# Neighbourhood attention: five score banks, three value banks whose results are copied out, and strict groups of products

## The chip, the cores and the metric

The kernel runs on one core of one Trainium2 chip. The metric is the device time of one execution in microseconds. The kernel before took 3622.86 us in the median of three runs (3616.02 to 3626.13).

A core has a matrix engine (TensorE, PE in the profile, with its weight loads shown apart as PEld), a vector engine (VectorE, DVE), a scalar engine (ScalarE, ACT), a general engine (GpSimd, POOL) and DMA queues, one fed by SyncE (SP) and one by GpSimd. Each engine runs its own instructions in their order and waits for others through semaphores. TensorE writes its products into PSUM, of which this kernel uses eight banks of 128x512 float32 in the stage in question; everything else lies in SBUF.

## What is computed

The reference is a two-layer backbone over 2048 latent tokens on a grid of 32 rows by 64 columns, with 256 context tokens in front. Layer 0 has latent attention and gated linear attention. Layer 1, with the stage in question, is neighbourhood attention with 16 heads of 64:

```python
def neighborhood_attention(q, k, v, k_ctx, v_ctx, rpb):
    ...
    def one_row(args):
        qr, r = args
        r_start = jnp.clip(r - kr // 2, 0, rows - kr)
        kb = lax.dynamic_slice_in_dim(kg, r_start, kr, axis=1)
        vb = lax.dynamic_slice_in_dim(vg, r_start, kr, axis=1)
        ...
        s_lat = jnp.einsum('bqhd,brkhd->bhqrk', qr, kb, preferred_element_type=jnp.float32) * scale
        s_lat = s_lat + bias.astype(jnp.float32)[None]
        s_lat = jnp.where(col_mask[None, None, :, None, :], s_lat, -jnp.inf).reshape(bsz, h, GRID_W, kr * GRID_W)
        s_ctx = jnp.einsum('bqhd,bchd->bhqc', qr, k_ctx, preferred_element_type=jnp.float32) * scale
        p = jax.nn.softmax(jnp.concatenate([s_lat, s_ctx], axis=-1), axis=-1).astype(v.dtype)
        o = jnp.einsum('bhqk,bkhd->bqhd', p[..., :kr * GRID_W], vb.reshape(bsz, kr * GRID_W, h, d))
        return o + jnp.einsum('bhqc,bchd->bqhd', p[..., kr * GRID_W:], v_ctx)
```

Every query sees a window of 8 by 16 latent tokens around it, with a bias table and a mask, and all 256 context tokens. The output is gated, projected and added to the stream.

## The kernel before, in words

The change touches `odd_attention` alone. It works through eight head pairs j; heads 2j and 2j+1 sit side by side in the partitions of the result.

A head pair has 20 steps. A context step ("c", n) makes the scores of the 512 queries of block n against the 256 context tokens: four products pairs (lines 1540 and 1541, the second of which adds the low parts and the maximum), one PSUM bank "st" each, and ACT takes the Exp out of each bank into an SBUF tile "opt". A latent step ("l", n) takes 128 latent keys against the rectangle of queries that can see them: two banks, one for each head; DVE adds the bias table out of the bank into an "opt" tile (line 1701, two or more rectangles for a tile), and ACT takes the Exp in place. The order of the steps is c0, c1, l0 to l3, c2, l4 to l7, c3, l8 to l15.

Every step has a tail, appended to a list `pend`. When six stand there, `flush(4)` runs the four oldest. A context tail opens a value bank "o" with eight products (line 1552) and DVE adds its two halves into the sums of the denominator (line 1560, two adds of 128x512, both inputs in SBUF). A latent tail adds value products into one or two value banks (line 1570), and POOL adds the tile into the sums (line 1576). The tail products are issued behind the last score product that stands before them; the score products after a flush are not tied to it, so the scheduler can place them among the tails.

The latent steps 7, 11 and 15 complete blocks 0, 1, and 2 with 3. Each completed block is put into `late` with a count of 2, and at the end of the second flush counted from there `finish_block` calls `finish` (lines 884 to 900): two products sum the denominators into a bank of the "st" ring (line 889); ACT takes Ln into "rl" and Exp into "rc"; DVE runs three operations of 128x512 (line 894 multiplies in the bank, line 895 writes the refined reciprocal into "rc", line 896 multiplies the value bank by it); the POOL queue stores the result (line 899).

Between the steps stand loads on the SP queue (keys by chunks of 512 tokens, queries, tables, values of the next head pair) and, at step 10, the masking of the next head pair's two tables by POOL (line 1533, two operations of 128x1034), issued behind the last POOL add at that place.

The "st" ring has four banks and the "o" ring four; they are all eight. In the last head pair the steps also split the output weights (`out_s`), and the projection of the first output tile (`first`) is woven in between the last flushes. The output projection follows.

Of the kernel before, what the change touches and what calls it, by code (L numbers as in the profile page):

```python
# [13 lines left out]
ALU = mybir.AluOpType  # L14
# [3 lines left out]
P = 128  # L18
# [70 lines left out]
class Kern:  # L89
# [1379 lines left out]
    def odd_attention(self, out, right, left, wout):  # L1469
# [4 lines left out]
        with ExitStack() as es:  # L1474
# [5 lines left out]
            for g in range(4):  # L1480
                steps += [("l", 4 * g + c) for c in range(4)]
                if g < 2:
                    steps.append(("c", g + 2))
            bank = lambda: self.tl(pp, [P, 512], "st", bufs=4)
            exps = lambda shape=[P, 2, 512], dt=F32: self.tl(ep, shape, "opt", dt, bufs=11)

            def qtile(j, i, part):
# [57 lines left out]
                return [acc[bb // 2][:, i].rearrange("p r c -> p (r c)")[:, (bb % 2) * 512 : (bb % 2) * 512 + 512] for i in range(2)]  # L1545

            def tail_ctx(n, pts, j, V, O, acc):
                O[n] = self.tl(pp, [P, 8, 64], "o", bufs=4)
                o = O[n][:].rearrange("p r c -> p (r c)")
                for u in range(2):  # L1550
                    for i in range(2):
                        mm = nc.tensor.matmul(o[i * 64 : i * 64 + 64, :], V[:, u, i * 64 : i * 64 + 64], pts[i][:, u, :],  # L1552
                                              start=u == 0, stop=False, skip_group_check=True)
                if n % 2 == 0:
                    if n == 0 and j % 2 == 0:
                        acc[0] = self.tl(left, [P, 2, 16, 64], "wo0", bufs=1)
                    else:
                        acc[n // 2] = self.tl(rp, [P, 2, 16, 64], f"oacc{n // 2}", bufs=1)
                for i, a in enumerate(sums(acc, n)):
                    nc.vector.tensor_tensor(out=a, in0=pts[i][:, 0, :], in1=pts[i][:, 1, :], op=ALU.add)  # L1560
                return mm

            def tail(n, pts, j, V, O, acc):
                g, c = divmod(n, 4)
                (r0, nr), (c0, w) = rect("k", g, c)
                done = {7: [0], 11: [1], 15: [2, 3]}.get(n, [])
                for bb in range(r0 // 8, (r0 + nr - 1) // 8 + 1):
                    a0, a1 = max(r0, bb * 8), min(r0 + nr, bb * 8 + 8)
                    for i in range(2):
                        mm = nc.tensor.matmul(O[bb][i * 64 : i * 64 + 64, a0 - bb * 8 : a1 - bb * 8, c0 : c0 + w],  # L1570
                                              V[:, NCT + n, i * 64 : i * 64 + 64], pts[:, i, a0 - r0 : a1 - r0, :],
                                              start=False, stop=bb in done, skip_group_check=True)
                for hf in range(r0 // 16, (r0 + nr - 1) // 16 + 1):
                    a0, a1 = max(r0, hf * 16), min(r0 + nr, hf * 16 + 16)
                    a = acc[hf][:, :, a0 - hf * 16 : a1 - hf * 16, c0 : c0 + w]
                    self.psum = nc.gpsimd.tensor_tensor(out=a, in0=a, in1=pts[:, :, a0 - r0 : a1 - r0, :], op=ALU.add)  # L1576
                late.extend([2, bb, j, O, acc] for bb in done)
                return mm

            def finish_block(bb, j, O, acc):  # L1580
                return self.finish(O.pop(bb)[:].rearrange("p r c -> p (r c)"), sums(acc, bb), None,
                                   self.RT1[j, :, bb * 512 : bb * 512 + 512], 512, fp, pp, ("st", 4), lp, (2, 3), nc.gpsimd)

            def weights():

# [50 lines left out]
            pend, late, OA = [], [], {}  # L1636
            all_k, most_k = slice(0, KD), slice(0, KD - 1)

            def flush(n):

                mm = None
                for f, *a in pend[:n]:
                    mm = f(*a)
                del pend[:n]
                for x in late:
                    x[0] -= 1
                for x in [x for x in late if x[0] <= 0]:
                    late.remove(x)
                    rc = finish_block(*x[1:])
                    if x[1:3] == [0, 7]:  # L1650
                        k = KD - 1
                        nc.gpsimd.tensor_tensor(out=r0[:, k, :], in0=rc[:, :P], in1=z0[:, k, :], op=ALU.mult)
                        self.project_split(r0[:, k, :], hi0[:, k, :], lo0[:, k, :])
                return mm

            for j in range(8):
                OA[j] = {}, {}
                for s, (kind, n) in enumerate(steps):
# [18 lines left out]
                    pts = exps() if kind == "l" else [exps(), exps()]  # L1677
                    if s in CHUNK and (j, s) not in ((0, 0), (7, 16)):
                        kt.append(chunk(j + (s == 16), CHUNK[s]))
                    for i in range(2):  # L1680
                        q1, q2 = Q[j, i]
                        if kind == "c":
                            for u in range(2):
                                ps = bank()
                                ks, qs = slice(u * P, u * P + P), slice(n * 512, n * 512 + 512)
                                mm = scores(ps[:], kc[j][0][:, i, ks], kc[j][1][:65, i, ks], q1[:, qs], q2[:65, qs])
                                ex = self.act(pts[i][:, u, :], ps[:], AF.Exp)
                            continue
                        k1, k2 = (k[:, i, c * P : c * P + P] for k in kt[0])
                        (r0_, nr), (c0, w) = rect("k", g, c)  # L1690
                        ps = bank()
                        a, m, d = even(c0, w)
                        pt = pts[:, i, : nr * w].rearrange("p (r c) -> p r c", r=nr)
                        ps = ps[:, : nr * m].rearrange("p (r c) -> p r c", r=nr)
                        q1, q2 = (q[:].rearrange("d (r c) -> d r c", r=32)[:, r0_ : r0_ + nr, a : a + m] for q in (q1, q2))
                        mm = scores(ps, k1, k2[:65], q1, q2[:65])
                        ps = ps[:, :, d : d + w]
                        for ro, ri, rn in pieces("k", 0, g, r0_, nr):
                            for co, ci, cn in pieces("k", 1, c, c0, w):
                                d = slice(ro, ro + rn), slice(co, co + cn)  # L1700
                                nc.vector.tensor_tensor(out=pt[:, d[0], d[1]], in0=ps[:, d[0], d[1]],  # L1701
                                                        in1=tabs[j][i][:, ri : ri + rn, ci : ci + cn], op=ALU.add)
                    if kind == "l" and c == 3:
                        kt.pop(0)
                    if kind == "l":
# [18 lines left out]
                        self.project_split(r0[:, most_k, :], hi0[:, most_k, :], lo0[:, most_k, :])  # L1724
                    if len(pend) == 6:
                        with self.tc.issue_after(mm.ins):
                            flush(4)
            for _ in out_s:
                pass
            y = lambda: self.tl(fp, [P, 512], "rc", bufs=3)  # L1730
# [144 lines left out]
```

## Time and profile before

| | |
|---|---|
| Median of three runs | 3622.86 us |
| The profiled execution | 3621.41 us |
| its span | 3619.6 us |
| its mean granted TensorE clock | 0.987 |
| Layer 1 attention in it | about 3032 to 3425 us |
| Output projection in it | from there to the end |

The page gives each engine's busy time and its share of the span. The windows give the same for a stretch: start and end, length, then busy time with the number of records for each engine, the granted clock of TensorE (1.00 is full), the busy share of the DMA engines and what they moved. A row of the timeline has its start, its length (of a run of like instructions where several are joined), engine, line, operation, result and operands, shape, and the count; the idle time before it and what ended it stand in brackets. A row of the waits has the engine, what it was about to write and the line, what it waited for, then the total in us, how many times, and the longest. A row of the groups has the form, the count, the busy time, the mean of one in ns, and the idle time before. Matmuls are pipelined, so neighbouring rows overlap, and the pace is read from start to start.

### The profile page before, as it was taken

The numbers are of one execution on the slowest core, as the hardware profiler recorded it, in microseconds if no ns is written. First come the engines' busy times: TensorE is split into PE (matmuls) and PEld (weight loads), VectorE is DVE, ScalarE is ACT, GpSimd is POOL, SyncE is SP. The second block draws the span as 40 slices with busy tenths as digits, with TensorE's granted clock in tenths as the row PEclk, the third lists the DMA queues.
The fourth block names the chain that finished last, engine by engine and source line by source line (L and its number), as shares of the span: only waits on it lengthen the run. The fifth ranks groups of instructions, "written<-read, shape, count | busy, mean of one in ns | idle before, by whom it ended". The sixth has DMA issues, their size and how long they took to land. (4 is left out here: it accounts for less than half of the span.)

```text
span 3619.6 us, 51689 instructions
## 1 busy us (share of the span) xinstructions
PE 3525.1 (97%) x18260; PEld 2737.6 (76%) x18260; DVE 2377.0 (66%) x4876; ACT 1429.4 (39%) x2705; POOL 1213.9 (34%) x1346
## 2 busy tenths in 40 slices
PE   8999999999999999999999999999999999999898
PEld 6988998888886666656667878888888886555577
DVE  4677665888886676697664344454587874677821
ACT  5545551111115555556553134444422223555510
POOL 1433430111011222212312233333444445677743
PEclk9999999999999999999999999999999999999999
DMA  7555462222243342424524544456644438778654
GB/s 253 151 155 155 140 197 92 90 76 84 72 115 83 91 108 72 108 79 134 157 89 144 172 158 129 144 147 192 212 139 127 131 124 205 210 210 221 185 178 145
DMA packets 396428, 513.63 MB, mean 142 GB/s; under 512 B 61229, under 2 KB 275197, under 8 KB 390266
## 3 DMA queue, kind: packets, MB, share of 16 engines
q1 hardware_dynamic: 358282, 426.94, 40.9%
q0 software_dynamic: 20512, 58.02, 5.6%
q10 hardware_dynamic: 17376, 25.37, 2.0%
q8 instruction: 145, 2.38, 0.3%
q14 instruction: 113, 0.93, 0.1%
HBM read 330.61 MB, written 179.59 MB: 141 GB/s over the span
## 5 line engine op out<-in xcount | busy, mean ns | idle before, releaser
L1007 DVE TENSOR_TENSOR acc<-acc,apt 128x512 f32<-128x512 f32 x512 | 376.0, 763 | 152.8 <-ACT apt L106 149.2
L666 DVE TENSOR_REDUCE mm<-mx 128x1 f32<-128x512 f32 (+1 forms) x656 | 393.0, 629 | 91.3 <-PE mx L665 83.1
L106 ACT ACTIVATE apt<-st 128x512 f32<-128x512 f32 (+1 forms) x592 | 342.9, 593 | 269.4 <-PE st L1018 224.4
L958 PE MATMUL av<-apt,av 128*64 128x512 f32 (+1 forms) x1184 | 269.2, 592 | 0.0
L1016 PE MATMUL st<-aq,akh 97*128 97x512 f32 x576 | 246.7, 428 | 0.6 <-ACT apt L106 0.6
L665 PE MATMUL mx<-mk,mq 96*128 96x512 f32 (+1 forms) x656 | 238.9, 373 | 0.0
L1017 PE MATMUL st<-aq,akh 96*128 96x512 f32 x576 | 229.1, 398 | 0.0
L1018 PE MATMUL st<-aq,akl 96*128 96x512 f32 x576 | 228.5, 397 | 0.0
L1443 DVE CUSTOM_DVE_ANT_1 mx<-mx,mtab 128x465 f32<-128x465 f32 (+14 forms) x576 | 184.0, 339 | 49.0 <-PE mx L1437 33.9
L106 ACT ACTIVATE opt<-opt 128x930 f32<-128x930 f32 (+9 forms) x144 | 119.1, 829 | 240.9 <-POOL opt L1741 136.4
L106 ACT ACTIVATE u<-gm 128x352 f32<-128x352 f32 (+1 forms) x144 | 70.3, 495 | 358.0 <-PE gm L131 207.4
L1701 DVE TENSOR_TENSOR opt<-st,tab 128x64 f32<-128x64 f32 (+10 forms) x576 | 143.3, 316 | 84.8 <-PE st L1541 47.4
L958 PEld LDWEIGHTS av<-apt,av 128*64 128x64 f32 x1184 | 79.8, 137 | 152.0 <-issue 149.7
L1576 POOL TENSOR_TENSOR oacc<-oacc,opt 128x682 f32<-128x682 f32 (+9 forms) x144 | 173.2, 1227 | 38.3 <-ACT opt L106 37.1
L1016 PEld LDWEIGHTS st<-aq,akh 97*128 97x128 f32 x576 | 108.9, 189 | 72.8 <-issue 43.4
L665 PEld LDWEIGHTS mx<-mk,mq 96*128 96x128 f32 x656 | 122.9, 189 | 11.7
L1018 PEld LDWEIGHTS st<-aq,akl 96*128 96x128 f32 x576 | 110.1, 191 | 25.2
L1540 PE MATMUL st<-q,kt 128*128 128x480 f32 (+5 forms) x256 | 100.3, 394 | 24.6 <-DVE opt L1701 20.0
L1017 PEld LDWEIGHTS st<-aq,akh 96*128 96x128 f32 x576 | 110.5, 192 | 17.6
L106 ACT ACTIVATE x<-px,modB,modA 128x128 f32<-128x128 f32 x272 | 99.1, 468 | 59.3 <-PE px L335 37.0
L129 PE MATMUL gm<-w0h,hhi 128*128 128x512 f32 x288 | 115.6, 401 | 2.3 <-DVE hhi L347 2.3
L129 PE MATMUL gm<-w1h,hhi 128*128 128x512 f32 x288 | 116.6, 405 | 0.0
(585 smaller groups left out, 9922.9 us busy)
## 6 DMA issues: line engine op xcount, KB each, us to landing
q<-Q SPq DMA_DIRECT2D x48, 512.0 KB
H<-x ACTq DMA_DIRECT2D x36, 512.0 KB
adaw<-ada_w SPq DMA_DIRECT2D x64, 256.0 KB
x<-H SPq DMA_DIRECT2D x32, 512.0 KB
K1t<-okt POOLq DMA_DIRECT2D x32, 512.0 KB, 6.7
kt<-K1t SPq DMA_DIRECT2D x32, 512.0 KB
mtab<-rpb_q SPq DMA_DIRECT2D x16, 899.0 KB
QT<-qkhl SPq DMA_DIRECT2D x36, 384.0 KB
```

The costliest lines, as they stand in the source:

```text
L106: return self.nc.scalar.activation(out, in_, func, **kw)
L129: self.nc.tensor.matmul(out, lh(k), rh(k), start=j == 0, stop=False)
L665: mm = nc.tensor.matmul(ps[:, :w], q[:A_QK, (t % 6) * P : (t % 6) * P + P], k[:A_QK, k0 : k0 + w], start=True, stop=True)
L666: nc.vector.tensor_reduce(out=m[:, t, n : n + 1], in_=ps[:, :w], axis=AX.X, op=ALU.max)
L958: nc.tensor.matmul(O[j, nb][i * 64 : i * 64 + 64, :w], V[j, kt // TT][:, kt % TT, i * 64 : i * 64 + 64], pts[i][:, :w], start=n == 0, stop ...
L1007: self.add = nc.vector.tensor_tensor(out=acc[i][:, :w], in0=a[:, :w], in1=pts[i][:, :w], op=ALU.add)
L1016: nc.tensor.matmul(ps[:, :w], kh[: A_QK + 1, i, kq], qh[: A_QK + 1, :w], start=True, stop=False)
L1017: nc.tensor.matmul(ps[:, :w], kh[:A_QK, i, kq], ql[:A_QK, :w], start=False, stop=False)
L1018: mm = nc.tensor.matmul(ps[:, :w], kl[:A_QK, i, kq], qh[:A_QK, :w], start=False, stop=True)
L1443: nc.vector.tensor_tensor_reduce(out=s, in0=s, in1=tb[:, ri : ri + rn, ci : ci + cn], scale=1.0, scalar=-3e38, op0=ALU.add, op1=ALU.max, a ...
L1576: self.psum = nc.gpsimd.tensor_tensor(out=a, in0=a, in1=pts[:, :, a0 - r0 : a1 - r0, :], op=ALU.add)
L1701: nc.vector.tensor_tensor(out=pt[:, d[0], d[1]], in0=ps[:, d[0], d[1]], in1=tabs[j][i][:, ri : ri + rn, ci : ci + cn], op=ALU.add)
```

## The change

Four things change. The rings: five "st" banks and three "o" banks. The end of a block: with its last value product ACT copies the value bank into an "rc" tile, and the bank is free for the next block; the denominator is worked on at the start of the next flush, in one "st" bank that the first two DVE operations rewrite in place, and the third multiplies the copy. The groups: the first scores after a flush are tied to the flush's last product (`behind`), and the first flush of all runs three tails, so that later groups end with l7, l11 and l15, the last product of a block; a flush of one tail is added after the loop. The tiles of the first output tile's projection come from the ring "rl".

In the order of the instructions that results, DVE has the two adds of c2 (line 1560) just behind the table adds of l5, and POOL has the table masks (line 1533) behind l3's add and ahead of those of l4; before, they stood behind l4's adds. The order of the loads on the SP queue is the same.

```diff
-            bank = lambda: self.tl(pp, [P, 512], "st", bufs=4)
+            bank = lambda: self.tl(pp, [P, 512], "st", bufs=5)
...
-                O[n] = self.tl(pp, [P, 8, 64], "o", bufs=4)
+                O[n] = self.tl(pp, [P, 8, 64], "o", bufs=3)
...
-                late.extend([2, bb, j, O, acc] for bb in done)
+                for bb in done:
+                    r = self.tl(fp, [P, 512], "rc", bufs=3)
+                    self.act(r[:], O.pop(bb)[:].rearrange("p r c -> p (r c)"))
+                    late.append((bb, j, r, acc))
                 return mm
 
-            def finish_block(bb, j, O, acc):
-                return self.finish(O.pop(bb)[:].rearrange("p r c -> p (r c)"), sums(acc, bb), None,
-                                   self.RT1[j, :, bb * 512 : bb * 512 + 512], 512, fp, pp, ("st", 4), lp, (2, 3), nc.gpsimd)
+            def finish_block(bb, j, r, acc):
+                den = bank()
+                for h, a in enumerate(sums(acc, bb)):
+                    nc.tensor.matmul(den[h * 64 : h * 64 + 64, :], self.mtwos[:], a, start=True, stop=True)
+                q = self.tl(lp, [P, 512], "rl", bufs=2)
+                self.act(q[:], den[:], AF.Ln, scale=-1.0)
+                self.act(q[:], q[:], AF.Exp, scale=-1.0)
+                nc.vector.tensor_tensor(out=den[:], in0=den[:], in1=q[:], op=ALU.mult)
+                nc.vector.scalar_tensor_tensor(out=den[:], in0=den[:], scalar=2.0, in1=q[:], op0=ALU.add, op1=ALU.mult)
+                nc.vector.tensor_tensor(out=r[:], in0=den[:], in1=r[:], op=ALU.mult)
+                nc.gpsimd.dma_start(self.RT1[j, :, bb * 512 : bb * 512 + 512], r[:])
+                return r
...
             def flush(n):
 
                 mm = None
+                for x in late:
+                    rc = finish_block(*x)
+                    if x[:2] == (0, 7):
+                        k = KD - 1
+                        nc.gpsimd.tensor_tensor(out=r0[:, k, :], in0=rc[:, :P], in1=z0[:, k, :], op=ALU.mult)
+                        self.project_split(r0[:, k, :], hi0[:, k, :], lo0[:, k, :])
+                late.clear()
                 for f, *a in pend[:n]:
                     mm = f(*a)
                 del pend[:n]
-                for x in late:
-                    x[0] -= 1
-                for x in [x for x in late if x[0] <= 0]:
-                    late.remove(x)
-                    rc = finish_block(*x[1:])
...
+                    es2 = ExitStack()
+                    if behind is not None:
+                        es2.enter_context(self.tc.issue_after(behind.ins))
+                        behind = None
                     for i in range(2):
...
+                    es2.close()
...
                     if len(pend) == 6:
                         with self.tc.issue_after(mm.ins):
-                            flush(4)
+                            behind = flush(3 if (j, s) == (0, 5) else 4)
+            with self.tc.issue_after(mm.ins):
+                mm = flush(1)
...
-            steps_of = lambda o, hi, lo, x: self.project_steps(hi, lo, x, gate, wout, bank, y, out[o * P : o * P + P, :])
-            first = steps_of(0, hi0, lo0, x0)
+            steps_of = lambda o, hi, lo, x, y=y: self.project_steps(hi, lo, x, gate, wout, bank, y, out[o * P : o * P + P, :])
+            first = steps_of(0, hi0, lo0, x0, lambda: self.tl(lp, [P, 512], "rl", bufs=2))
```

More of the change, by code (lines that the diff above doesn't have):

```diff
@@ L1635, in odd_attention @@
             out_w, out_s = weights(), split()
-            pend, late, OA = [], [], {}
+            pend, late, OA, behind = [], [], {}, None
             all_k, most_k = slice(0, KD), slice(0, KD - 1)
@@ L1644, in flush @@
                 del pend[:n]
-                for x in late:
-                    x[0] -= 1
-                for x in [x for x in late if x[0] <= 0]:
-                    late.remove(x)
-                    rc = finish_block(*x[1:])
[L1650 to L1653, printed above, removed]
                 return mm
```

## The prediction, made before the changed kernel ran

> **What bounds the kernel now.** I began with the page: TensorE (PE) is the bound of the whole span, and no other engine is near it.
>
> ```profile
> span 3619.6 us, 51689 instructions
> ...
> PE 3525.1 (97%) x18260; PEld 2737.6 (76%) x18260; DVE 2377.0 (66%) x4876; ACT 1429.4 (39%) x2705; POOL 1213.9 (34%) x1346
> ```
>
> The change touches the neighbourhood attention of layer 1 alone. In the timeline this runs from about 3032 to 3425 us, 8 head pairs one after the other. So I cut it at the same instruction of every head pair, the 48 value products that follow the last score group, and read the windows between those cuts.
>
> ```profile
> core 0: us, PE busy (x) PEld busy (x) DVE busy (x) ACT busy (x) POOL busy (x), PEclk, DMA share, GB/s
> 3076.10:3124.88 48.78, 46.86 (x305) 28.87 (x304) 30.26 (x89) 25.09 (x40) 31.63 (x28) 0.96 0.84 214
> 3124.88:3173.07 48.19, 46.28 (x306) 27.83 (x305) 32.76 (x94) 25.58 (x41) 34.74 (x31) 0.96 0.78 209
> 3173.07:3219.79 46.72, 44.81 (x307) 27.38 (x306) 35.47 (x94) 25.59 (x41) 32.73 (x30) 1.00 0.81 214
> 3219.79:3268.15 48.36, 46.43 (x305) 27.73 (x304) 32.63 (x94) 25.55 (x41) 36.12 (x32) 0.96 0.79 208
> 3268.15:3316.41 48.26, 46.35 (x306) 27.86 (x305) 32.71 (x94) 25.60 (x41) 34.67 (x31) 0.96 0.80 207
> 3316.41:3361.96 45.55, 44.04 (x306) 27.52 (x305) 35.63 (x94) 25.64 (x41) 32.55 (x29) 1.00 0.83 224
> 3361.96:3425.00 63.04, 54.16 (x367) 33.49 (x367) 55.72 (x124) 36.66 (x62) 44.24 (x40) 0.95 0.54 168
> ```
>
> Six steady head pairs take 47.64 us in the mean (3361.96 less 3076.10, over 6). Four show a granted clock of 0.96 and take 48.4 us in the mean; two show 1.00 and take 46.1. The last window is another case: VectorE (DVE) is busy 55.7 of 63.0 us there.
>
> "PE busy 96%" hides the loss, because pipelined ends overlap. I therefore compared, in the undisturbed head pair at 3173.07, the time of each stretch of score products with the columns in it.
>
> ```profile
> 3177.65 0.29 PE L1540 MATMUL st<-q,kt 128*128 128x264 f32 x1
> ...
> 3182.11 0.40 PE L1540 MATMUL st<-q,kc 128*128 128x512 f32 x1
> 3182.35 0.39 PE L1541 MATMUL st<-q,kc 65*128 65x512 f32 x1
> 3182.58 0.40 PE L1540 MATMUL st<-q,kc 128*128 128x512 f32 x1
> ...
> 3183.14 2.28 PE L1570 MATMUL o<-opt,ov 128*64 128x72 f32 x32
> 3185.25 1.03 PE L889 MATMUL st<-wo,mtwos 128*64 128x512 f32 x4
> 3186.21 0.40 PE L1540 MATMUL st<-q,kt 128*128 128x288 f32 x1
> ...
> 3190.79 1.94 PE L1552 MATMUL o<-opt,ov 128*64 128x512 f32 x8
> ...
> 3199.54 0.32 PE L1540 MATMUL st<-q,kt 128*128 128x360 f32 x1
> ...
> 3203.13 1.32 PE L1570 MATMUL o<-opt,ov 128*64 128x248 f32 x16
> ...
> 3216.15 0.49 PE L1540 MATMUL st<-q,kt 128*128 128x480 f32 x1
> ...
> 3219.78 3.02 PE L1570 MATMUL o<-opt,ov 128*64 128x72 f32 x48
> ```
>
> A pair of score products (L1540 and L1541) of 512 columns repeats every 0.47 us (3182.11 to 3182.58), 0.92 ns a column. One head pair has 20064 columns of scores (16 context tiles of 512; 32 latent tiles of 264 to 480), so 18.4 us at that pace. The stretches take longer. 3186.21 to 3190.79 is 4.58 us for 2688 columns, worth 2.5: 2.1 lost, with a denominator bank (L889) held. 3199.54 to 3203.13 is 3.59 us for 2640 columns, worth 2.4: 1.2 lost. 3216.15 to 3219.78 is 3.63 us for 2912 columns, worth 2.7: 1.0 lost. Counted so, the score stretches of this head pair lose 7.1 us, the turns from one kind of work to the other included; 46.72 less 7.1 leaves 39.6 us of work. The waits name who holds the bank.
>
> ```profile
> PEld st L1540 <- issue: 4.3, 9, 0.8
> PEld st L1540 <- PE st L1541: 3.6, 7, 0.8
> ...
> PE st L1540 <- DVE opt L1701: 1.5, 4, 0.5
> PEld st L1540 <- ACT opt L106: 1.2, 3, 0.5
> PEld st L1540 <- PE st L889: 0.8, 1, 0.8
> ```
>
> A score product waits for the DVE add of the table (L1701) or the Exp (L106) that empties a bank of the ring of four. The issue waits, 9 of them, are mostly the turns from value products back to scores, some 0.3 us each.
>
> **The change, part by part.** *A fifth score bank, and groups that are strict.* The static order of PE shows, per head pair, exactly five score groups and five tail groups of four steps; the order before turns seven times from values to scores. Two turns less are 0.6 us of the sum below. With letters for the new groups (scores, then what holds banks there): A = latent 9 to 12, nothing held; B = latent 13 to 15 and context 0, one denominator bank held; C = context 1, latent 0 to 2, nothing; D = latent 3, context 2, latent 4 and 5, nothing; E = latent 6, 7, context 3, latent 8, two denominator banks held. Groups A, C and D are like the stretches that lose 1.0 to 1.2 with four banks; with a fifth I take a third off: 0.7 each. B is like the stretch that lost 2.1, with four banks free where that had three: 1.7. E has three free, but its context step needs no DVE: 1.8, between 0.7 (denominators done early) and 4.1 (all six DVE operations ahead of its adds, 6 times 0.68). Sum 5.5, the five turns included, against 7.1 with seven: -1.5 us per head pair, rounded down, from -2.7 (E at 0.7) to +0.7 (E at 4.1).
>
> *The copy.* ScalarE (ACT) gets four copies of 128x512 from PSUM per head pair. No such copy is in the trace; the nearest rows are two ACT operations of that size from PSUM.
>
> ```profile
> L106 ACT ACTIVATE rl<-st 128x512 f32<-128x512 f32 x29 | 17.2, 593 | 46.0 <-PE st L889 46.0
> L106 ACT ACTIVATE opt<-st 128x512 f32<-128x512 f32 x112 | 60.3, 603 | 29.9 <-PE st L1541 29.9
> L1560 DVE TENSOR_TENSOR oacc<-opt 128x512 f32<-128x512 f32 x44 | 47.1, 1082 | 0.1
> ```
>
> Four times 0.60 is 2.4 us on an engine busy 25.6 of 46.7: nothing on the path while that slack covers it; without it, 0.6 us behind each of three block ends, 1.8. What queues behind a copy is the next Exp, and behind that the value products of its step. The value bank comes free at the copy, so three are enough; the old order held it to L896, whose successor reads the copy. The "rc" ring has three buffers, so block 3's copy must wait until the store of block 0 has landed.
>
> ```profile
> RT<-rc POOLq DMA_DIRECT2D x29, 256.0 KB, 6.3
> ```
>
> Block 0 is stored in group A and block 3 copied at the end of group C, two groups later, some 18 us: 6.3 us of landing is hidden, price 0; uncovered it would hold ACT for the rest of a landing.
>
> *The denominators earlier.* They are issued one flush sooner. PE sees the same four products; what can be late is their sums, made by GpSimd (POOL, L1576) and by L1560. From 0 to 2 us per head pair; I take 0, since they stand behind three tails in the order of PE.
>
> *What moves beside GpSimd's masks.* In the order of DVE, the two adds of context step 2 (L1560) come just behind the table adds of latent 5; in POOL's order the masks (L1533) now stand before latent 4's adds, where before they were behind them.
>
> ```profile
> 3205.20 4.77 POOL L1533 TENSOR_TENSOR tab<-tab,maskk 128x1034 f32<-128x1034 f32 x2
> 3209.91 4.21 POOL L1576 TENSOR_TENSOR oacc<-oacc,opt 128x682 f32<-128x682 f32 x4
> ...
> 3210.81 3.87 DVE L1560 TENSOR_TENSOR oacc<-opt 128x512 f32<-128x512 f32 x1
> ...
> 3215.11 0.68 DVE L1560 TENSOR_TENSOR oacc<-opt 128x512 f32<-128x512 f32 x1
> ```
>
> The same add takes 0.68 us alone and 3.87 us beside four POOL operations that run back to back; the mean of 44 is 1.08. It ends within 0.6 us of the last of the four: it is shut out while POOL runs. Beside the masks, each of the two adds can wait for the rest of a mask of 2.4 us, 1.7 us more than alone, or for a whole train, 3.2 more; together 0 to 6.4. DVE has 11 us of slack in a head pair, yet the table adds of group E are queued behind these two. In the sum I take 0, as most adds run at 0.68; the rest is a rival. [...]
>
> *The rest.* The first flush, the extra one at the end and the "rl" tiles of the first output tile: once each, under 1 us. The first head pair and the last gain little: the last is bound by DVE. So 6 head pairs and half of one more: 6.5 times -1.5 is -9.8 us.
>
> *The clock.* The four head pairs at 0.96 are 2.3 us longer than the two at 1.00.
>
> ```profile
> 3142.92 3.10 PE L1552 MATMUL o<-opt,ov 128*64 128x512 f32 x8
> ```
>
> The same eight products take 1.94 us in the row at 3190.79: a stretch at a lower clock, right behind the score group that loses 2.1 us. That group's tiles fall into C and D, which lose less; B and E remain as triggers. I let two of the four go: -4.6, between -9.2 and +4.6 (all six). [...]
>
> Sum: 3619.6 + 1.8 around it = 3621.4; less 9.8 and 4.6 gives 3607.0. This run lies 1.5 us under the median of the runs shown.
>
> **The rivals.** *The lock (B).* The two adds of context step 2 meet the masks. For it: the new order of both queues, and the row of 3.87 us. Against it: DVE's slack, and most adds at 0.68. Price: one add waits for a mask (1.7), the other for a train (3.2), 4.9 us of DVE ahead of group E's table adds; 1.3 of it lies in waits that E has anyway, and 3.6 less the gain of 1.5 is +2.1 per head pair. The two head pairs without a dip then have one too: +4.6. 3621.4 + 6.5 times 2.1 + 4.6 = 3639.7, from 3626 (one mask only, 0.5 per head pair) to 3652 (4 us). It decides from the point where the two adds cost 2.8 us of DVE, 1.5 and the 1.3.
>
> *Strict groups give it back (C).* The order before could fill a wait for a bank with value products; the strict one cannot. For it: the loss gathers in B and E, each behind denominators. E at 3.3 instead of 1.8 takes the whole gain: 3621, from 3613 to 3636. Against it: the group that lost 1.2 had no denominator at all, only four banks.
>
> *ACT waits for a store (D).* The fourth copy waits for a landing, and ACT's Exps behind it. Against it: 18 us where 6.3 are needed. Were the landing 4 us late, 4 less 1.5 is 2.5 per head pair: 3638.
>
> **How the numbers follow.** A, the forecast, 0.45, own range 3594 to 3614; B 0.42; C 0.09; D 0.04. A measurement of this kernel can tell about 0.3%, 11 us, from no change: faster is under 3612, slower over 3634. A lies under 3612 nine times in ten: 0.41. B lies over 3634 four times in five, D nearly always, C one time in ten: 0.39. The rest is 0.20. The range 3588 to 3644 leaves out a little of A (all dips gone and more than 2 us per head pair) and three tenths of B, under 2 in 10.
>
> **What would show it.** Right: steady head pairs of 45 to 46.5 us, a granted clock of 1.00 in more of them, seven turns from values to scores become five, L1540's waits on L1701 smaller per head pair. The lock: L1560's mean well over 1.08 us, with DVE rows of 2 to 4 us beside L1533. C: waits on L889's banks and on L1701 in groups B and E that add up to 5 us or more. D: an ACT copy waiting for the store. I am wrong if the steady head pair stays at 47.6 or more with L1560 unchanged, or if the time moves outside the attention, which the change should leave alone.

## The result, and the profile after

The changed kernel is slower. Its median over six runs is 3635.32 us (3631.99 to 3644.48) against 3620.46 us for the kernel before in the same series; the ratio is 1.0044, 95% interval 1.0033 to 1.0055, some 16 us. The forecast was 3607. The profiled execution has a span of 3633.0 us, 13.4 more than before.

The windows of the changed kernel, cut at the start of group E (latent 6) of six head pairs in a row; columns as in the prediction.

```profile
core 0: us, PE busy (x) PEld busy (x) DVE busy (x) ACT busy (x) POOL busy (x), PEclk, DMA share, GB/s
3109.71:3162.58 52.87, 49.23 (x306) 32.77 (x305) 32.46 (x94) 27.88 (x45) 34.30 (x31) 0.87 0.71 190
3162.58:3210.36 47.78, 45.17 (x305) 29.34 (x304) 31.34 (x92) 27.59 (x45) 33.87 (x30) 0.96 0.80 210
3210.36:3260.53 50.17, 46.80 (x306) 30.44 (x305) 31.90 (x94) 27.59 (x45) 33.87 (x30) 0.93 0.75 200
3260.53:3306.46 45.93, 43.61 (x306) 28.51 (x305) 31.29 (x92) 27.48 (x45) 33.19 (x30) 1.00 0.81 214
3306.46:3356.73 50.27, 46.14 (x306) 30.70 (x305) 32.89 (x93) 27.65 (x45) 34.29 (x31) 0.93 0.73 199
3356.73:3406.11 49.38, 46.07 (x306) 31.00 (x305) 37.35 (x96) 29.88 (x49) 33.08 (x30) 0.93 0.57 176
```

Six head pairs take 296.40 us, 49.4 each. Before, six successive starts of the nearest stretch (second half of latent 7, 3112.49 to 3396.27) gave 47.3 each. That is +2.1 a head pair where -1.5 was forecast, +12.6 over six, nearly the whole difference of the spans. One head pair (45.93) is faster than the mean before: the kernel can do it, and in most head pairs something stops it. ScalarE is busy 27.6 us instead of 25.6: the copies take 2.0 us where 2.4 was priced. The lower clock, 0.87 to 0.96, is in five of six.

The pace of the prediction (0.92 ns a column) applied to every score stretch of the changed kernel gives the loss by group, in us, for the head pairs in order (a group that a head pair cuts differently is left out):

```
A  latent 9-12                    0.24 in each but the first (3.72)
B  latent 13-15, context 0'       2.0 in each
C  context 1', latent 0'-2'       0.24 in each
D  latent 3, context 2, latent 4-5   3.96 4.12 2.41 3.36 1.49 1.52 0.98
E  latent 6-7, context 3, latent 8   0.21 4.49 1.98 2.39 1.98 5.14 4.64 6.64
```

A fifth bank does more than forecast in A and C, where no denominator holds one (0.24 against 0.7); B is near its 1.7. The loss is in D and E, and it varies from one head pair to the next. The waits of the stage name two that were not there before. The kernel before, then the changed kernel:

```profile
PE st L1540 <- DVE opt L1701: 20.0, 34, 3.5
...
PEld st L1540 <- DVE opt L1701: 7.8, 11, 2.7
```

```profile
DVE oacc L1560 <- PE st L1586: 28.6, 6, 6.2
...
PE st L1540 <- DVE opt L1715: 25.5, 20, 3.3
...
PEld st L1540 <- DVE opt L1715: 15.9, 15, 3.5
...
ACT rc L106 <- DMA RT<-rc: 10.4, 6, 2.3
```

(L1715 is the table add, L1701 before; L1586 the denominators' products, L889 before; L1590 to L1592 their three operations.) The waits of score products for the table adds have grown from 20.0 and 7.8 us to 25.5 and 15.9. Behind them stand the two new ones: VectorE stands 28.6 us before the adds of a context step, for the products of a denominator; ScalarE stands 10.4 us before a copy, for a store. The timeline of the changed kernel shows the second in the head pair where D loses 3.96.

```profile
3084.50 0.57 POOL L1593 DMA_DIRECT2D RT<-rc  x1
...
3090.90 0.60 ACT L106 ACTIVATE rc<-o 128x512 f32<-128x512 f32 x1
3091.91 0.82 ACT L106 ACTIVATE opt<-opt 128x744 f32<-128x744 f32 x1 [0.41 <-DVE opt L1715]
3094.99 0.60 ACT L106 ACTIVATE rc<-o 128x512 f32<-128x512 f32 x1 [2.25 <-DMA RT<-rc]
...
3096.20 0.59 ACT L106 ACTIVATE rl<-st 128x512 f32<-128x512 f32 x1
3096.82 0.63 ACT L106 ACTIVATE rl<-rl 128x512 f32<-128x512 f32 x1
3097.48 0.70 DVE L1590 TENSOR_TENSOR st<-st,rl 128x512 f32<-128x512 f32 x1 [4.63 <-ACT rl L106]
3098.22 0.70 DVE L1591 SCALAR_TENSOR_TENSOR st<-st,rl 128x512 f32<-128x512 f32 x1
3098.82 0.85 DVE L1715 TENSOR_TENSOR opt<-st,tab 128x64 f32<-128x64 f32 x6
...
3099.60 0.72 PE L1540 MATMUL st<-q,kc 128*128 128x512 f32 x1 [1.95 <-DVE opt L1715]
```

Read it backwards. TensorE waits 1.95 us for a bank; the bank waits for latent 3's table adds; these stand on VectorE behind L1590 and L1591; those wait for Ln and Exp of block 1's denominator; and these stand on ScalarE behind the copy of block 3, which waits 2.25 us until the store issued at 3084.50 (block 0) has left the buffer. The store alone takes long on this chain, 10.4 us from issue to landing; the rest is four queues, each in its own order. The first product after it takes 0.72 us where 0.40 to 0.50 is usual: the granted clock has gone down too, to 0.51 from 3099.60 to 3102.60.

The first wait, in the head pair whose E loses 5.14:

```profile
3301.71 4.72 POOL L1533 TENSOR_TENSOR tab<-tab,maskk 128x1034 f32<-128x1034 f32 x2
...
3304.86 0.59 PE L1586 MATMUL st<-oacc,mtwos 128*64 128x512 f32 x1
...
3305.58 3.14 DVE L1560 TENSOR_TENSOR oacc<-opt 128x512 f32<-128x512 f32 x2 [3.88 <-PE st L1586]
...
3306.39 1.77 POOL L1576 TENSOR_TENSOR oacc<-oacc,opt 128x528 f32<-128x528 f32 x1
...
3308.64 0.68 DVE L1590 TENSOR_TENSOR st<-st,rl 128x512 f32<-128x512 f32 x1
...
3309.24 1.17 DVE L1715 TENSOR_TENSOR opt<-st,tab 128x465 f32<-128x465 f32 x2
...
3309.92 0.43 PE L1540 MATMUL st<-q,kt 128*128 128x360 f32 x1 [1.97 <-DVE opt L1715]
```

Context 2 opens the sums of blocks 2 and 3. Their buffer (oacc1, one only) still holds the sums of the head pair before, until the denominators' products have read it; in the new order these stand behind the tails of group D, after context 2's first value products. So its two adds, and all of VectorE behind them, start at 3305.6 beside GpSimd's masks and the add that the masks pushed back, and take 3.14 us where two take 1.3. Latent 6's table adds come 1.8 us later still, and TensorE waits 1.97.

### The profile page after: what moved, and what is told of

It reads as the page before. It is cut to its first block, busy times and chain, and to the rows that moved or that the text cites. A ratio compares the mean times of both kernels' runs of the same rounds, so it can differ in the third digit from the quotient of the medians.

```text
span 3633.0 us, 51686 instructions
## 1 busy us (share of the span) xinstructions
PE 3530.4 (97%) x18260; PEld 2756.3 (76%) x18260; DVE 2365.1 (65%) x4876; ACT 1446.2 (40%) x2737; POOL 1207.2 (33%) x1346
## 4 chain that ended last, share of the span: by engine, by line
PE 68%; issue 15%; DMA 6%; DVE 5%; POOL 4%; ACT 2%; SPq 0%; POOLq 0%; DVEq 0%; ACTq 0%
PE av L958 7%; PE gm L129 7%; PE gm L131 7%; PE gm L130 7%; PE st L1016 4%; PE st L1017 4%; PE st L1018 3%; PE o L1570 2%; PE st L129 2%; PE st L131 2%; PE st L130 2%; PE st L1540 1%; PE pj L129 1%; PE pj L131 1%; PE pj L130 1%
## 5 line engine op out<-in xcount | busy, mean ns | idle before, releaser
L106 ACT ACTIVATE opt<-opt 128x930 f32<-128x930 f32 (+8 forms) x144 | 118.7, 830 | 239.2 <-POOL opt L1758 136.5
L1715 DVE TENSOR_TENSOR opt<-st,tab 128x64 f32<-128x64 f32 (+10 forms) x576 | 143.3, 314 | 33.2 <-PE st L1541 32.1
L1018 PEld LDWEIGHTS st<-aq,akl 96*128 96x128 f32 x576 | 110.3, 192 | 25.5
L206 POOL TENSOR_TENSOR oss<-oss,mhalf 128x8 f32<-128x8 f32 x68 | 113.1, 1663 | 5.5
```

What stands on the lines that cost most here:

```text
L106: return self.nc.scalar.activation(out, in_, func, **kw)
L1018: mm = nc.tensor.matmul(ps[:, :w], kl[:A_QK, i, kq], qh[:A_QK, :w], start=False, stop=True)
```

## The experiments

Theories: S, the wait for the store (in D); W, the wait of context 2's adds for the denominators (in E); L, that W is harmless by itself and only moves the adds to where they meet GpSimd (E); and G, that the strict groups and the banks held by denominators cost the time. Each kernel is compared with the kernel before on the same chip. Group losses are worked out as above, from one execution of each kernel; E is the mean of head pairs 1 to 6. That execution can lie off the median (3634.3 us for e1_rc4, 3623.5 for e4_nobehind), so means of E that differ by a few tenths say little.

| | edit | median us | ratio to before, 95% | D, mean | E, mean |
|---|---|---|---|---|---|
| changed kernel | | 3635.3 | 1.0044 (1.0033 to 1.0055) | 2.55 | 3.44 |
| e1_rc4 | fourth rc buffer | 3630.7 | 1.0021 (1.0009 to 1.0033) | 0.39 | 4.39 |
| e2_rot | sums in turn | 3629.3 | 1.0026 (1.0016 to 1.0035) | 1.95 | 2.98 |
| e3_rot_rc4 | both | 3611.3 | 0.9973 (0.9963 to 0.9983) | 0.39 | 1.98 |
| e4_nobehind | no tie | 3632.8 | 1.0026 (1.0015 to 1.0037) | cut otherwise | 3.28 |
| e5_best_st4 | e3, four score banks | 3674.7 | 1.0149 (1.0131 to 1.0168) | 1.13 | 3.67 |
| e6_best_nobehind | e3, no tie | 3623.7 | 1.0010 (1.0000 to 1.0020) | cut otherwise | 4.87 |
| e7_rc4_mask13 | e1, late masks | 3609.2 | 0.9968 (0.9956 to 0.9980) | 0.40 | 1.98 |
| e8_rings | before, rings and copy alone | 3621.5 | 1.0004 (0.9993 to 1.0016) | other groups | other groups |
| e9_mask13 | changed kernel, late masks | 3623.1 | 1.0006 (0.9995 to 1.0016) | 2.48 | 1.98 |
| e10_best_mask13 | e3, late masks | 3638.9 | 1.0050 (1.0035 to 1.0066) | 0.40 | 1.82 |

**The store.**

```diff
-                    r = self.tl(fp, [P, 512], "rc", bufs=3)
+                    r = self.tl(fp, [P, 512], "rc", bufs=4)
...
-            y = lambda: self.tl(fp, [P, 512], "rc", bufs=3)
+            y = lambda: self.tl(fp, [P, 512], "rc", bufs=4)
```

> The changed kernel with a fourth buffer in the ring that takes the copies (rc). Theory S (the copy of block 3 waits on ScalarE for the store of block 0, six times 1.3 to 2.3 us, and the next denominator's Ln and, on VectorE, its two operations and the table adds of latent 3 queue behind it): these waits vanish, the score group with context 2 loses 1 us instead of 1 to 4, and the time falls by 8 to 14 us, to 3621 to 3627. Theory G (the strict groups and the banks held by denominators cost the time, the wait is only seen there): the wait vanishes and the time stays at 3632 to 3638.

The wait is gone, and D falls from 2.55 to 0.39 us in the mean, in six of seven head pairs to 0.30: S is the whole of D's loss, the lower clock that came with the wait included. The time falls by 0.0023 only, 8 us, where D alone gives 7 times 2.16, 15 us; the rest is given back in E, which now loses 4.6 in five head pairs of six. Without the ragged wait for the store the second add of context 2 takes 1.8 us beside GpSimd in all six head pairs, where in the changed kernel it does so in three. One head pair of the six shows how much of the loss is the clock. The first row is from a group E that loses 4.58, the second from the one that loses 3.27:

```profile
3215.83 0.62 PE L1540 MATMUL st<-q,kt 128*128 128x360 f32 x1 [1.42 <-DVE opt L1715]
...
3263.72 0.43 PE L1540 MATMUL st<-q,kt 128*128 128x360 f32 x1 [1.43 <-DVE opt L1715]
```

The adds (2.59 and 2.60 us for the two) and the wait are the same; behind the first the context products start 0.42 us apart, behind the second 0.24, and the head pairs' windows (from 3212.91 and from 3260.79) show a granted clock of 0.93 and 1.00. So 1.3 us of the 4.6 are the clock, and the same wait comes with a dip in five head pairs and with none in that one. The median lies between what S and G expected.

**The sums.**

```diff
-                    if n == 0 and j % 2 == 0:
-                        acc[0] = self.tl(left, [P, 2, 16, 64], "wo0", bufs=1)
-                    else:
-                        acc[n // 2] = self.tl(rp, [P, 2, 16, 64], f"oacc{n // 2}", bufs=1)
+                    tag = "oacc1" if (j, n) == (7, 2) else ("wo0", "oacc1", "oacc0")[(2 * j + n // 2) % 3]
+                    acc[n // 2] = self.tl(left if tag == "wo0" else rp, [P, 2, 16, 64], tag, bufs=1)
```

> The changed kernel with the three SBUF sums of the denominators used in turn, so that context 2 of a head pair no longer writes the sums that the last denominators of the head pair before still read (the last head pair keeps the old buffer). Theory W (VectorE stands 28.6 us in all before the adds of context 2, until the products of the denominators of blocks 2 and 3 have read the buffer, and the table adds of latent 6 and 7 queue behind): this wait shrinks to that of the last head pair, the group with context 3 loses 2 us instead of 2 to 5, and the time falls by 6 to 12 us, to 3623 to 3629. Theory G: the two denominators hold their banks as before, and the time stays at 3632 to 3638.

The wait for L1586 is gone from the list, yet E only falls from 3.44 to 2.98 in the mean. The edit also moves the adds in VectorE's order: one of the two now stands ahead of latent 4's table adds, the other ahead of latent 5's (with a fourth buffer too, between latent 5's). The second meets an add of GpSimd and takes 1.8 us in five of six head pairs, but this is not what E loses: with it E loses 1.9 in two of them and 3.4 to 3.7 in the others. In E these two kinds have the same waits (0.55 and 0.44 us for table adds in the head pairs at 3109.73 and 3156.20, which lose 1.9 and 3.5); the lossy ones run the rest of the group at the lower clock, and their windows show 0.90 to 0.96. Why the clock falls in four and not in two, this run does not show. A gain of 0.0018, just short of W.

> Both edits. Theories S and W together: 15 to 25 us less than the changed kernel, 3610 to 3620, level with the kernel before or faster. If both waits stem from one cause, no more than the larger of the two alone. Theory G: 3632 to 3638.

Both edits gain 0.0071, 26 us, more than the sum of the single ones (0.0041), and the kernel is faster than before. Its windows, cut as those above:

```profile
3108.84:3153.72 44.88, 43.46 (x306) 29.11 (x305) 31.69 (x93) 27.40 (x45) 34.24 (x31) 1.00 0.84 225
3153.72:3198.61 44.89, 43.48 (x305) 29.12 (x304) 31.67 (x93) 27.48 (x45) 34.28 (x31) 1.00 0.86 224
...
3288.38:3334.79 46.41, 44.99 (x306) 30.18 (x305) 31.63 (x93) 27.48 (x45) 34.21 (x31) 0.96 0.79 216
3334.79:3379.49 44.70, 42.99 (x305) 28.62 (x304) 34.98 (x94) 29.76 (x49) 32.20 (x30) 1.00 0.68 196
```

Five of the six take 44.7 to 44.9 us at the full clock; the other has a granted clock of 0.96 and takes 1.5 us more. That is how two edits give more than their sum: with one of the waits left, four (e2_rot) or five (e1_rc4) of six windows lie under 1.00, with both gone one does. G is out as the cause of the loss: groups and denominators stand as in the changed kernel. Since the sums in turn also move the two adds, this run does not part the wait from the place of the adds; the next does.

**The masks.** Which part of W costs? The masks of the next tables (L1533) moved from step 10 to step 13, in the kernel with four rc buffers:

```diff
                         elif s == 13:
+                            with self.tc.issue_after(self.psum.ins):
+                                mask(tabs[j + 1], mk)
                             V[j + 1] = values(j + 1)
...
-                        elif s == 10:
-                            with self.tc.issue_after(self.psum.ins):
-                                mask(tabs[j + 1], mk)
```

> The kernel with four rc buffers alone, with the masks of the next tables (GpSimd) at step 13 instead of 10, behind the adds of latent 7. Lock theory: the two adds of context 2, which there start behind the denominators and take 0.86 and 1.81 us beside the masks, take 0.68 each, and the group with context 3 loses 3 to 3.5 us instead of 4.6: 7 to 12 us off, 3619 to 3624. Rival (the wait for the denominators alone makes the loss): 3627 to 3633, the group still at 4.3 or more.

The waits of this kernel still hold the one for the denominators:

```profile
DVE oacc L1560 <- PE st L1586: 23.3, 6, 3.9
```

It is 23.3 us, to the tenth what it is in e1, and VectorE's order around the adds is the same; E loses 1.98 instead of 4.39. So W alone is nearly free (1.97 against 1.81 in the five undisturbed head pairs of e3_rot_rc4, whose mean of 1.98 has the one with the dip in it), and L is right: what costs is that the adds, made late, run beside GpSimd. In its timeline the two adds take 1.29 us together:

```profile
3202.42 1.29 DVE L1560 TENSOR_TENSOR oacc<-opt 128x512 f32<-128x512 f32 x2 [3.88 <-PE st L1586]
```

against 2.59 in e1, in the timeline of that kernel:

```profile
3212.03 2.59 DVE L1560 TENSOR_TENSOR oacc<-opt 128x512 f32<-128x512 f32 x2 [3.88 <-PE st L1586]
```

Of the 2.6 us that E loses less (1.97 where five head pairs of e1 lose 4.6), 1.3 are these; the other 1.3 go with the clock, 0.93 in five of six windows of e1 and 1.00 in five of six here. The one E of e1 at the full clock, 3.27, lies 1.3 above 1.97 and says the same. The gain, 0.0053 or 19 us, is more than the theory expected for that reason.

> The changed kernel (three rc buffers, sums as they were) with the masks at step 13 alone. If the two costs, the copy's wait for the store and the adds that meet the masks, stand side by side: the group with context 3 loses 2.0 as in the kernel with four rc buffers and late masks, the group with context 2 keeps its 1 to 4, and the time is 3618 to 3628. If the masks are all of it: 3607 to 3613. If late masks help only together with the fourth buffer: 3630 or more.

As expected for two costs side by side: E at 1.98, D at 2.48 as in the changed kernel, 3623.1 us. With e1, e7 and the changed kernel this makes a square: late masks alone -0.0038, the fourth buffer alone -0.0023, both -0.0076. That both give more than the sum is here within the noise (0.0015, with intervals of some 0.001 on each of the four ratios).

> Sums in turn, four rc buffers and the masks at step 13. If moving the masks and using the sums in turn remove the same collision: no more than either, 3605 to 3614, the group with context 3 at 1.8 to 2.0. If they remove different waits: under 3604.

Neither: it is as slow as the changed kernel (1.0050 and 1.0044, with overlapping intervals). With the sums in turn context 2's adds come early and need no late masks; at step 13 the masks meet the adds of context 3 instead, in every steady head pair. Group A, 0.24 in the steady head pairs of the other kernels with five banks and these groups, loses 3.9. Its timeline:

```profile
3116.74 5.36 DVE L1558 TENSOR_TENSOR wo<-opt 128x512 f32<-128x512 f32 x1
3116.81 4.72 POOL L1533 TENSOR_TENSOR tab<-tab,maskk 128x1034 f32<-128x1034 f32 x2
...
3119.74 0.33 PE L1541 MATMUL st<-q,kt 65*128 65x360 f32 x1
...
3122.02 1.18 DVE L1712 TENSOR_TENSOR opt<-st,tab 128x465 f32<-128x465 f32 x2
...
3122.70 0.67 PE L1540 MATMUL st<-q,kt 128*128 128x360 f32 x1 [2.64 <-DVE opt L1712]
```

One add (L1558 here) ends 0.6 us after the end of both masks; the table adds behind it start at 3122.0, and TensorE, which has filled five banks by 3120.1, waits 2.64 us. This is the collision by itself, without any wait for a denominator or a store.

**The tie.**

```diff
-                    if behind is not None:
+                    if False:
```

> The changed kernel without the tie of the first scores after a flush to the flush's last product, so that the scheduler may place scores among value products again. Theory G (strict groups cost the time): 3615 to 3624. Theories S and W: the waits for the store and for the denominators stay as long as the denominators stand where they do, and the time is within 5 us of 3635.

3632.8, as S and W expected; the waits for the store (11.0 us) and for the denominators (24.9) are there as in the changed kernel.

> The kernel with both edits, without the tie of the first scores to the last product of the flush. If strict groups are neutral once the two waits are gone: 3605 to 3616. If strictness is a part of the gain (fewer turns, fewer stretches at a lower clock): over 3618. If it is a cost: under 3603.

Over 3618: once the two waits are gone, the tie is worth 0.0037 of the time, 13 us. Group E loses 4.87 in each of six head pairs, and the timeline of VectorE in one of them says how:

```profile
3151.25 2.64 DVE L1558 TENSOR_TENSOR oacc<-opt 128x512 f32<-128x512 f32 x1
...
3156.64 0.70 DVE L1588 TENSOR_TENSOR st<-st,rl 128x512 f32<-128x512 f32 x1 [2.20 <-ACT rl L106]
3157.38 0.70 DVE L1589 SCALAR_TENSOR_TENSOR st<-st,rl 128x512 f32<-128x512 f32 x1
3157.98 0.69 DVE L1588 TENSOR_TENSOR st<-st,rl 128x512 f32<-128x512 f32 x1
3158.58 0.68 DVE L1590 TENSOR_TENSOR rc<-st,rc 128x512 f32<-128x512 f32 x1
3159.18 0.63 DVE L1713 TENSOR_TENSOR opt<-st,tab 128x465 f32<-128x465 f32 x1
```

(L1588 to L1590 are the denominators' operations here, L1713 the table add, L1558 the add of a context step.) Without the tie VectorE's own order changes, and four of the six denominators' operations stand ahead of latent 6's first table add. The prediction had priced E at 4.1 with all six ahead; this is nearly that case, in a run whose mean granted clock is 0.982 (0.987 in e3_rot_rc4). The second add of context 2 meets the masks as well (2.64), but VectorE is idle again before the denominators, so that is not what E waits for.

**The banks.** 

> The kernel with both edits (sums in turn, four rc buffers), but with four score banks instead of five, one bank of PSUM left unused. If the fifth bank carries the gain: the groups that lose 0.24 us lose about 1 again, as with four banks before, those with denominators about 3, and the time is 3623 to 3640. Rival (the groups wait on the order of VectorE, not on the number of banks): 3608 to 3616.

With one bank idle the kernel is 63 us slower than with five, more than expected, and it isn't the banks alone. The groups other than E lose 3.2 us more than in e3 (A 0.70, B 3.6, C 0.59, D 1.13 in the mean, less 0.24, 1.99, 0.24 and 0.39): 21 us over six and a half head pairs. That is the most that this run gives for a bank, for the run's mean granted clock is 0.976 (0.987 in e3_rot_rc4), and VectorE's order differs too: as in e6_best_nobehind, four of the denominators' operations stand ahead of latent 6's first table add. For the rest the timeline shows the masks again:

```profile
3210.47 6.72 DVE L1558 TENSOR_TENSOR oacc<-opt 128x512 f32<-128x512 f32 x1 [0.62 <-ACT opt L106]
...
3211.95 4.69 POOL L1533 TENSOR_TENSOR tab<-tab,maskk 128x1034 f32<-128x1034 f32 x2
...
3217.85 3.39 PE L1584 MATMUL st<-oacc,mtwos 128*64 128x512 f32 x8 [3.79 <-DVE opt L1713]
```

In five head pairs one add of context 2 is shut out for 6.7 us, through an add of GpSimd and both masks, and the denominators' products wait 3.79 us for a bank that the table adds behind it would free. What each of these is worth alone was not measured.

> The kernel before with the rings and the copy alone: five score and three value banks, the copy to one of four rc buffers, the denominators still at the end of the second flush, flushes of four, no tie. If the rings give the gain by themselves: its stretches of scores lose 4 to 5 us per head pair instead of 7.1, 3603 to 3613. If the gain needs the groups that end with a block: within 5 us of 3621. If the copy itself costs ScalarE: over 3626.

Level with before. The rings and the copy alone do not give the gain: some stretches lose less (1.0 to 2.0 us where the one with a denominator lost 2.1), but the one with context 2 and latent 4 to 6 loses 2.6 where, cut in two, it lost some 1.5 before, and the time of a head pair, 47.5 and 47.6 us in two windows, is that of before, with a clock of 0.96 in both. Which wait stands behind the 2.6 was not followed.

## Why the prediction was wrong, point by point

**Five banks and the turns**: right in kind, too small. A and C 0.24 (forecast 0.7), B 2.0 (1.7), five groups as read from the order. With the two waits removed (e3) D is 0.39 and E 1.98, and the groups sum to 4.8 us against the 5.5 forecast (its own terms add up to 5.6); six head pairs then take 45.1 us in the mean, 2.2 less than before. The forecast, 1.5 and some 0.7 of clock a head pair, holds for a kernel without the two waits. One reading of the order was wrong without harm: D does hold a denominator's bank, block 1's (its products run at 3092.73, just ahead of D), and loses 0.3 with it once the store is out of the way, so a held bank by itself does not cost what B's 2.0 suggested.

**The copy's own time**: right, 2.0 us more on ScalarE, off the path.

**The store**: here the first step failed. "Block 0 is stored in group A and block 3 copied at the end of group C, two groups later, some 18 us: 6.3 us of landing is hidden, price 0". Two numbers of it were wrong, and it took both. First, the margin is 8.2 us, not 18. The tails that end with l7 run behind E, and the denominator is worked on at the start of the next tails, behind A; so its operations fall into B, and the store, behind the third of them and behind GpSimd's adds, is issued at the end of B (3084.50). Block 3's copy comes early in the tails behind C, since l15 is the first of them (of the groups of tails only the one with l7 ends with a block's last product; l11 and l15 begin theirs). It is wanted at 3092.7. Second, the landing takes 10.4 us here and 9.5 to 10.4 in the six head pairs that wait, not 6.3. That number was a median over all the stores of the kernel before, where block 0's own landed in 8.7 to 9.8; in the changed kernel the median is longer too:

```profile
RT<-rc POOLq DMA_DIRECT2D x28, 256.0 KB, 7.8
```

With 6.3 the buffer would have been free 1.9 us before the copy. The price in D was 2.2 us per head pair (2.55 less 0.39). Rival D named this mechanism and held it for unlikely; it took the landing to be 4 us late, where the copy waited 1.3 to 2.3.

**The denominators earlier**: "I take 0, since they stand behind three tails in the order of PE". For their own sums they are early enough. What was not looked for is who waits for them: the buffer of the sums is single, and context 2 of the next head pair writes it. In the order before, the same products stood ahead of that tail. By itself this wait, 28.6 us in all, costs next to nothing (e7_rc4_mask13); it makes the adds late.

**The masks**: here the second step failed: "In the sum I take 0, as most adds run at 0.68". Rival B had the place and the operations, but not the size: E loses 3.44 instead of 1.98, 1.5 us where B's price was 3.6, and in the worst head pairs the two adds take 1.8 us more than alone (3.14 against 1.3), not 4.9 (the lower end of B's times, 3626, is 3625 by its own terms). Its sign, a mean of L1560 well over 1.08 us, did not come either; one of the adds takes 1.8 us or more in three of the six head pairs only:

```profile
L1560 DVE TENSOR_TENSOR oacc<-opt 128x512 f32<-128x512 f32 x44 | 42.1, 970 | 36.3 <-PE st L1586 28.6 <-ACT opt L106 7.6
```

e10 shows an add shut out for two masks, 4.7 us longer than alone, inside the 0 to 6.4 of the text. What B did not have is why they meet: with the sums in turn they miss each other, though narrowly (e3), and it takes W to bring them together, or a bank less (e5), or the missing tie (e6). That B's +2.1 a head pair and 3640 us lie close to the measured +2.1 and 3635 is luck: more than half of the loss is the store's, which B does not contain. What the prediction calls the lock is, in the runs, an add that is kept out while GpSimd works, for 3.87 us in the row of before and 5.36 in e10, and in e10 behind more than one operation: the last 0.13 us of an add of GpSimd, then both masks. What keeps it out, no run shows.

**The clock**: two of four dips were to go. There are more of them: five of six windows under 1.00, one at 0.87. In e3 one of six remains. Where waits went, most dips went, as the text assumed; in the changed kernel the waits did not get smaller. But a dip does not follow from a wait alone: the same waits came with one and without one in e1 (1.42 and 1.43 us) and in e2 (0.55 and 0.44 us in both).

**The rest**: "under 1 us" is borne out by the profiled executions: outside the six head pairs the changed kernel loses 0.8 us (13.4 in all less 12.6), e3 0.4 (12.7 gained in all, 13.1 in the six). Group E of the last head pair loses 6.6 us in every kernel with these groups; it was not examined.

So the range held the time, but the sum had the wrong sign: -1.5 us per head pair forecast, +2.1 measured, by two costs that were set to zero (D +2.2, E +1.5), the clock that came with them included.

## What to carry to other kernels

When instructions are reordered, follow each buffer that they free to its next writer, queue by queue, with the times at which each queue gets there: the banks gained were real, and were lost to a copy queued behind a store and to sums queued behind a product. Where two engines shut each other out, as VectorE's adds and GpSimd's masks did here, it is the moment at which long trains meet that counts (an add begun 0.11 us before the masks took 0.69 us in e3, one begun 0.07 us before them 5.36 in e10), so a change that only shifts one of them by a microsecond can gain or lose more than it does by itself; try its neighbours (the masks at another step, the sums in another buffer), and do not stack two cures for one collision (e3 3611.3 us, e7 3609.2, both cures in e10 3638.9). Take the landing of a store from the stores at that place, not from the median of all (9.5 to 10.4 us here, where the median was 7.8). A wait in this stage cost more where the granted clock fell after it (in e1 the group with a wait of 1.42 us and a clock of 0.93 lost 4.58, the one with 1.43 us and 1.00 lost 3.27), so such costs need not add up.

## What the runs showed of the hardware

An add of 128x512 with both inputs in SBUF, 0.68 us alone, took 5.36 us beside two masks of 2.4 us each that ran back to back on GpSimd, behind an add that ended 0.13 us after it began; it was not let in between them; in e5 6.72 us beside three. GpSimd pays as well: its add of 128x528, 1.32 us in the kernel with both edits, took 1.77 beside such an add. Who gets in at a boundary is not the same each time. In e3's timeline

```profile
3191.79 1.26 POOL L1574 TENSOR_TENSOR wo<-wo,opt 128x552 f32<-128x552 f32 x1 [0.98 <-ACT opt L106]
...
3192.91 0.69 DVE L1558 TENSOR_TENSOR oacc<-opt 128x512 f32<-128x512 f32 x1
3193.02 5.17 POOL L1533 TENSOR_TENSOR tab<-tab,maskk 128x1034 f32<-128x1034 f32 x2
```

the add begins 0.1 us before the masks, gets in, and the masks take 0.45 us longer; in e10 it begins 0.07 us before them and stays out for both. In both an add of GpSimd was still running when it began. What decides it, no run here shows.

A store of 256 KB on GpSimd's queue took 9.5 to 10.4 us to land at one place of the head pair, where the median of all was 7.8. And the granted clock did not follow from the wait before it alone: behind waits of 1.42 and 1.43 us for the same table adds in e1, products of 512 columns started 0.42 us apart in one head pair (clock 0.93) and 0.24 in another (1.00). The two single cures, 0.0023 and 0.0018, gave 0.0071 together, with the granted clock at 0.93 in five of six windows of the first and at 1.00 in five of six of the pair.
